# Seven-product units for the first two input blocks of the up projections, with turned blocks gated by wider operations

## The chip, the cores and the metric

The kernel runs on one core of one Trainium2 chip. The metric is the device time of one execution in microseconds, the median over runs. Alongside it there is one profiled execution, from which the profile's page and trace come. The engines are named as the profile names them: PE (TensorE, matrix products), PEld (its weight loads), DVE (VectorE), ACT (ScalarE), POOL (GpSimd) and SP (SyncE, which here only issues DMAs).

## The reference

Two decoder layers over 256 tokens of width 2048, in float32. Each layer has a mixer and then a gated feed-forward part; the change touches only the feed-forward part, which runs once in each layer:

```python
D_MODEL = 2048; SEQ = 256; DEPTH = 2
FFN_HIDDEN = 5632                       # 44 blocks of 128; w_up has 2 * 5632 columns

def conv_ffn(h, w_up, conv_w, conv_b, w_down):
    seq = h.shape[1]
    z = h @ w_up
    zp = jnp.pad(z, ((0, 0), (CONV_WIDTH - 1, 0), (0, 0)))
    z = sum(conv_w[j] * zp[:, j:j + seq] for j in range(CONV_WIDTH)) + conv_b
    a, b = jnp.split(z, 2, axis=-1)
    return (jax.nn.silu(a) * b) @ w_down

    # in each layer: x = x + mixer(...);  h = rms_norm(x, ffn_norm[l]);  x = x + conv_ffn(h, ...)
```

So there are 2048 x 11264 weights up and 5632 x 2048 weights down in each layer, a causal convolution of width 3 along the tokens in between (three taps and a bias for each of the 11264 columns), and the product of the silu of one half with the other half.

## The kernel before, in words

**Products.** Every large product is done with operands split in two: a weight tile `w` of 128 x 1024 values arrives by DMA (SP issues it), ACT writes its rounded part `wh` (line 186), and DVE writes the rest, `wl = w - wh` (line 187). Activations are kept split the same way. One product is then three matmuls: high by high, high by low, low by high (lines 380, 382, 383). A weight tile covers four blocks of 128 output columns and two input blocks of 128 rows; below it is called a piece. For a piece PE runs 12 matmuls of 512 columns: two halves of the tokens, two input blocks, three matmuls each. `project_four` runs through the pieces of one group of four output blocks: 8 pieces for an up projection (16 input blocks), 6 for a full step of the down projection (12 input blocks), into two banks of PSUM.

**Seven-product units.** The generator `seven` (lines 410 to 475) treats two groups of output blocks together, for the first two input blocks: a product of 2 x 2 blocks by 2 x 2 blocks made with 7 products instead of 8. With three matmuls a product, a unit has 21 matmuls where the two pieces it replaces have 24. It pays for that elsewhere. DVE makes sums and differences of the weights (lines 448 to 451, into the tiles `near` and `far`, named `sums` in the trace). Three and a half tiles are split into `wh` and `wl` instead of two. ACT copies one partial result from bank to bank (line 457) and one to the spare tile `p5` (line 462, `p` in the trace). DVE twice adds this spare to a bank (lines 465 and 470). Sums of the activations, made once for two input blocks by `combos` (lines 391 to 407, tile `comb`), must be ready. The second weight tile, `near` and `far` lie where the residual `x` was; `x` is sent to HBM from POOL's queue by the first `combine` of a layer, and fetched back behind the last unit (`x_back`). The generator is advanced one stage at a time between pieces of another projection: `project_four` takes it as `inset`, with the index of the first piece that a stage stands before. Before the change only the down projections use units: two for each of the three full steps, 6 in a layer.

**The feed-forward part.** `ffn` runs 11 up pairs (`up`): four blocks of the first half of the columns (`za`), then the matching four blocks of the second half (`zb`), each by `four`. `STEPS` says after how many up pairs a down step follows: 4 pairs, down over 12 hidden blocks, 3 pairs, down, 4 pairs, down, and a last down over the remaining 8 blocks. A down step has four groups of output blocks (`q` 0 to 3).

**After an up projection** the result has tokens in rows and must be turned. ACT evacuates the two banks into two `z` tiles (line 1422, with the norm's scale), DVE transposes 32 x 32 blocks within them into `tmp` (line 483), 16 DMAs, alternating between SP's and POOL's queues, carry the pieces to `zt` (line 492), and then `conv` works on each of the four turned blocks. ACT computes tap 2 and the bias (line 1436), DVE adds tap 1 and tap 0 (lines 1437 and 1438). For the `a` half ACT applies silu (line 98, tile `conv`); for the `b` half DVE multiplies by it (line 1460), ACT writes the rounded part of the hidden block (line 500) and DVE the rest (line 502).

**What sets the order.** These followers are generators. `tick()` advances all those in flight by one stage, once for each piece (and twice in a unit), so their instructions are sown between the pieces; the generator of a turned group waits 8 ticks (`LATE`) between the transposes' DMAs and `conv`. `held` keeps an instruction from being placed ahead of the latest `wh` or `wl`. A scheduler then fixes the order on each engine, and each engine works strictly in that order. ACT and DVE run ahead of PE as far as the buffers allow: `w` has 5 buffers and `wh` and `wl` have 3 each, with two more of each in a second pool that some pieces use.

## Time and profile before

| | |
|---|---|
| three runs | 2163.55, 2165.5, 2167.18 us; median 2165.5 |
| profiled execution | 2161.98 us, its span 2160.2 us, granted clock 1.000 |
| PE busy | 2152.4 us, 100%; 10700 matmuls recorded |
| PEld busy | 1887.7 us, 87% |
| DVE busy | 1683.7 us, 78%; 2451 instructions |
| ACT busy | 1338.6 us, 62%; 1942 instructions |
| DMA | 491.99 MB, mean 228 GB/s |

A row of the grouped view gives line, engine, operation, the tiles written and read, their shape, the count, then busy time and mean duration of one, then the idle time just before them on their engine and what ended it. The durations of neighbouring instructions overlap a little on DVE and ACT, and by almost half on PE: a matmul is shown with 379 ns, but the next starts after 216 ns. What a matmul costs is therefore read from the distance of starts.

### The profile page before, as it was taken

The numbers are of one execution on the slowest core, as the hardware profiler recorded it, in microseconds if no ns is written. First come the engines' busy times: TensorE is split into PE (matmuls) and PEld (weight loads), VectorE is DVE, ScalarE is ACT, GpSimd is POOL, SyncE is SP. The second block draws the span as 40 slices with busy tenths as digits, with TensorE's granted clock in tenths as the row PEclk, the third lists the DMA queues.
The fourth block names the chain that finished last, engine by engine and source line by source line (L and its number), as shares of the span: only waits on it lengthen the run. The fifth ranks groups of instructions, "written<-read, shape, count | busy, mean of one in ns | idle before, by whom it ended". The sixth has DMA issues, their size and how long they took to land.

```text
span 2160.2 us, 32319 instructions
## 1 busy us (share of the span) xinstructions
PE 2152.4 (100%) x10700; PEld 1887.7 (87%) x10700; DVE 1683.7 (78%) x2451; ACT 1338.6 (62%) x1942; POOL 476.6 (22%) x873
## 2 busy tenths in 40 slices
PE   9999999999999999999999999999999999999999
PEld 8888888888888888888888888888888888888888
DVE  7887768878677867787987787877878578858786
ACT  6677766666656645664565556766666566556652
POOL 0352231212012002111233443212211011011203
PEclk9999999999999999999999999999999999999999
DMA  8755778877777767777777766788786777677786
GB/s 302 224 169 174 224 223 266 250 228 221 231 225 226 216 217 209 249 218 239 243 236 228 241 207 209 224 255 252 235 247 203 229 224 228 217 214 216 223 281 186
DMA packets 494344, 491.99 MB, mean 228 GB/s; under 512 B 115584, under 2 KB 460304, under 8 KB 494048
## 3 DMA queue, kind: packets, MB, share of 16 engines
q1 hardware_dynamic: 466752, 457.60, 67.4%
q0 software_dynamic: 25984, 30.18, 5.8%
q10 hardware_dynamic: 1440, 2.15, 0.4%
q8 instruction: 84, 1.38, 0.3%
q14 instruction: 84, 0.69, 0.1%
HBM read 439.44 MB, written 6.31 MB: 206 GB/s over the span
## 4 chain that ended last, share of the span: by engine, by line
PE 94%; DVE 2%; DMA 1%; SPq 1%; ACT 1%; issue 1%; DVEq 0%; ACTq 0%
PE pm L382 15%; PE pm L380 15%; PE pm L383 15%; PE px L380 10%; PE px L382 10%; PE px L383 10%; PE pm L351 5%; PE pm L352 4%; PE pm L353 4%; PE pm L237 1%; PE pm L316 1%; SPq L492 1%; DVE wl L187 1%; PE pm L319 1%; PE pm L326 0%
## 5 line engine op out<-in xcount | busy, mean ns | idle before, releaser
L187 DVE TENSOR_TENSOR wl<-w,wh 128x1024 fp32r<-128x1024 f32 (+1 forms) x808 | 974.9, 1216 | 354.5 <-ACT wh L186 345.5
L186 ACT ACTIVATE wh<-w 128x1024 fp32r<-128x1024 f32 (+1 forms) x808 | 842.1, 1049 | 515.3 <-PE pm L383 206.2
L492 POOL DMA_DIRECT2D zt<-tmp x413 | 223.5, 549 | 1112.9 <-DVE tmp L483 908.6
L382 PE MATMUL pm<-wl,a 128*128 128x512 f32 x1024 | 388.4, 379 | 0.6 <-DVE wl L187 0.6
L380 PE MATMUL pm<-wh,a 128*128 128x512 f32 x1024 | 388.9, 380 | 0.0
L383 PE MATMUL pm<-wh,a 128*128 128x512 f32 x1024 | 388.1, 379 | 0.0
L380 PE MATMUL px<-wh,a 128*128 128x512 f32 x704 | 266.8, 379 | 0.0
L382 PE MATMUL px<-wl,a 128*128 128x512 f32 x704 | 266.8, 379 | 0.0
L383 PE MATMUL px<-wh,a 128*128 128x512 f32 x704 | 266.8, 379 | 0.0
L382 PEld LDWEIGHTS pm<-wl,a 128*128 128x128 f32 x1024 | 193.5, 189 | 28.6 <-DVE wl L187 1.5
L380 PEld LDWEIGHTS pm<-wh,a 128*128 128x128 f32 x1024 | 193.6, 189 | 27.5
L383 PEld LDWEIGHTS pm<-wh,a 128*128 128x128 f32 x1024 | 193.5, 189 | 27.4
L351 PE MATMUL pm<-wh,a 128*128 128x512 f32 x416 | 158.5, 381 | 0.0
L352 PE MATMUL pm<-wl,a 128*128 128x512 f32 x416 | 157.7, 379 | 0.0
L353 PE MATMUL pm<-wh,a 128*128 128x512 f32 x416 | 157.7, 379 | 0.0
L383 PEld LDWEIGHTS px<-wh,a 128*128 128x128 f32 x704 | 133.1, 189 | 18.9
L380 PEld LDWEIGHTS px<-wh,a 128*128 128x128 f32 x704 | 133.1, 189 | 18.9
L382 PEld LDWEIGHTS px<-wl,a 128*128 128x128 f32 x704 | 133.1, 189 | 18.9
L1436 ACT ACTIVATE conv<-zt,pp 128x256 f32<-128x256 f32 x176 | 100.1, 589 | 71.8 <-DMA zt<-tmp 54.9
L492 POOL DMA_DIRECT2D turn<-tmp x159 | 86.4, 551 | 189.5 <-DVE tmp L483 169.0
L1437 DVE SCALAR_TENSOR_TENSOR conv<-zt,pp,conv 128x255 f32<-128x255 f32 x176 | 83.1, 479 | 53.2 <-ACT conv L1436 44.8
L382 PE MATMUL px<-wl,hid 128*128 128x512 f32 x304 | 115.3, 379 | 0.2 <-DVE wl L187 0.2
(320 smaller groups left out, 3504.8 us busy)
## 6 DMA issues: line engine op xcount, KB each, us to landing
w<-in_w_up SPq DMA_DIRECT2D x352, 512.0 KB, 5.3
w<-in_w_dn SPq DMA_DIRECT2D x164, 512.0 KB, 5.2
w<-in_w_cqkv SPq DMA_DIRECT2D x96, 512.0 KB, 5.0
w<-in_w_abo SPq DMA_DIRECT2D x32, 512.0 KB, 4.8
w<-in_w_cg SPq DMA_DIRECT2D x32, 512.0 KB, 5.0
w<-in_w_co SPq DMA_DIRECT2D x32, 512.0 KB, 4.8
zt<-tmp SPq DMA_DIRECT2D x416, 32.0 KB, 2.3
zt<-tmp POOLq DMA_DIRECT2D x413, 32.0 KB, 2.3
```

What stands on the lines that cost most here:

```text
L186: r = deep["wh"] = SC.activation(wh, w, AF.Copy)
L187: deep["wl"] = V.tensor_tensor(wl, w, wh.bitcast(F32), ALU.subtract)
L237: deep["last"] = PE.matmul(to_two(ps[g][T]), a[:, o + T * P:o + (T + 1) * P], by_two(t, i), start=k + i + j == 0, stop=k + i == KT - 1 and ...
L351: PE.matmul(to_two(ps[T]), ah, h, start=k + i == 0, stop=False)
L352: PE.matmul(to_two(ps[T]), ah, l, start=False, stop=False)
L353: deep["last"] = PE.matmul(to_two(ps[T]), al, h, start=False, stop=k + i == KT - 1)
L380: PE.matmul(to_rows(ps[T]), ah, h, start=not begun and k + i == ks[0], stop=False, skip_group_check=loose)
L382: PE.matmul(to_rows(ps[T]), ah, l, start=False, stop=False, skip_group_check=loose)
L383: deep["mm"] = deep["last"] = PE.matmul(to_rows(ps[T]), al, h, start=False, stop=not more and k + i == ks[-1] + 1, skip_group_check=loose)
L492: queues[(a + b) % len(queues)].dma_start(dst[BLK * b:BLK * (b + 1), :, a * n:(a + 1) * n], tmp[BLK * a:BLK * (a + 1), b * 4 * n:(b + 1) * ...
L1436: held(SC.activation(c, z, AF.Identity, bias=pp[:, cb:cb + 1], scale=w(2)))
L1437: V.scalar_tensor_tensor(c[:, 1:], z[:, :S - 1], w(1), c[:, 1:], ALU.mult, ALU.add)
```

## The change

Two things are changed, both in `ffn`.

First, the up pairs use units too. From the third pair on, the first two input blocks of `za` and `zb` of a pair are computed together by one `seven` unit (`begin_up`), whose stages are inset into the `zb` projection of the pair before it, or into the last group of the down step before it. `four` then starts at the third input block, into the banks that the unit has begun. That is pairs 2 to 10, so 9 units a layer, 18 in the program. Since the tile `comb` has one buffer, the activation sums are made anew whenever the use goes from hidden blocks to the normed input or back: `combine(None)` is for the input, `combine(k)` for hidden blocks. That makes 6 a layer, where there were 3. The first `combine(None)` of a layer, which sends `x` away, now runs as soon as the norm's scale is known and no longer waits for hidden blocks. The units that start a down step stay as they were.

Second, what follows the turning is regrouped. ACT computes tap 0 of each block into `tmp` (new line 1437), which is free by then; DVE adds tap 1 for each block as before (now line 1438), and tap 0 for all four blocks by one addition of 4 x 254 columns (line 1440). Silu, the product with the other half (line 1462), the rounded part (line 1466) and the rest (line 1468) are each one operation on 4 x 256 columns. The `conv` tiles are now two of 1024 columns (before: six of 256), the hidden tiles five of four blocks (before: twenty of one).

```diff
-        def four(j0, inset=None):
-            ps = project_four(w_up[l, j0:j0 + 4], A, KT, inset=inset)
+        def four(j0, inset=None, ps=None):
+            ps = project_four(w_up[l, j0:j0 + 4], A, KT, ks=range(2 if ps else 0, KT, 2), ps=ps, inset=inset)
...
-        def conv(z, j, half):
...
-            c = hp.tile([P, S], F32, tag="conv", name=nm("conv"), bufs=6)
-            held(SC.activation(c, z, AF.Identity, bias=pp[:, cb:cb + 1], scale=w(2)))
-            V.scalar_tensor_tensor(c[:, 1:], z[:, :S - 1], w(1), c[:, 1:], ALU.mult, ALU.add)
-            V.scalar_tensor_tensor(c[:, 2:], z[:, :S - 2], w(0), c[:, 2:], ALU.mult, ALU.add)
+        def conv(z4, tmp, j):
+            c = hp.tile([P, 4, S], F32, tag="conv", name=nm("conv"), bufs=2)
+            far = tmp.rearrange("p (m t) -> p m t", m=4)
+            for i in range(4):
...
+                held(SC.activation(ci, z, AF.Identity, bias=pp[:, cb:cb + 1], scale=w[2]))
+                SC.activation(far[:, i], z, AF.Copy, scale=w[0])
+                V.scalar_tensor_tensor(ci[:, 1:], z[:, :S - 1], w[1], ci[:, 1:], ALU.mult, ALU.add)
+                yield
+            held(V.tensor_tensor(c[:, :, 2:], c[:, :, 2:], far[:, :, :S - 2], ALU.add), "wl")
             return c
...
-                for i in range(4):
-                    a = conv(za[:, i], j0 + i, 0)
-                    act(a, a, AF.Silu)
-                    ca.append(a)
-                    yield
+                a = yield from conv(za, ta, j0)
+                yield
+                held(act(a, a, AF.Silu))
+                ca.append(a)
...
-                for i in range(4):
-                    b = conv(zb[:, i], HT + j0 + i, 1)
-                    V.tensor_tensor(b, b, ca[i], ALU.mult)
-                    t = hp.tile([P, 512], F32R, tag="hid", name=nm("hid"), bufs=20)
-                    split(t, b, turn=True)
-                    hid.append(t)
-                    yield
+                b = yield from conv(zb, tb, HT + j0)
+                yield
+                held(V.tensor_tensor(b, b, ca[0], ALU.mult), "wl")
+                t = hp.tile([P, 4, 512], F32R, tag="hid", name=nm("hid"), bufs=5)
...
+                SC.activation(h, src, AF.Copy)
+                yield
+                held(V.tensor_tensor(lo, src, h.bitcast(F32), ALU.subtract), "wl")
+                hid.extend(t[:, i] for i in range(4))
...
-            yield from combos(t, hid[k:k + 2], hp.tile([P, 1024], F32, tag="tmp", name=nm("tmp"), bufs=2), None)
+            yield from combos(t, A[0:2] if k is None else hid[k:k + 2],
+                              hp.tile([P, 1024], F32, tag="tmp", name=nm("tmp"), bufs=2), None)
...
+        def begin_up(j):
+            return begin([w_up[l, o:o + 4] for o in (4 * j, HT + 4 * j)], None, lambda: A[0:2])
...
+                    elif q == 3 and after:
+                        coming, gen = begin_up(j0)
                         inset = (gen, 0, True)
...
-                    if after:
+                    if after:
+                        queue.append(combine(None))
+                    else:
                         x_back()
-                    else:
-                        queue.append(combine(k0 + n))
...
+            until = sum(n for n, _ in STEPS[:g + 1]) + ahead
+            while j0 < until:
+                now_begun, begun, inset = begun, (), None
+                if j0 + 1 == until:
+                    queue.append(combine(k0))
+                    begun, gen = begin_down(0, k0)
                     inset = (gen, 2, True)
-                up(4 * j0, inset)
+                elif j0:
+                    begun, gen = begin_up(j0 + 1)
+                    inset = (gen, 2, True)
+                up(4 * j0, inset, now_begun)
                 j0 += 1
```

The prediction speaks of three places in the order of instructions; they stand here before and after.

On PE, at the first two input blocks of an up group (`a_3572` and `a_3595`; `pm` and `px` are the PSUM banks): before, the third pair's `za` begins with a plain piece.

```order
L380 MATMUL pm_4777<-wh_4785,a_3572 128x512
L382 MATMUL pm_4777<-wl_4786,a_3572 128x512
L383 MATMUL pm_4777<-wh_4785,a_3572 128x512
L380 MATMUL pm_4777<-wh_4785,a_3595 128x512
L382 MATMUL pm_4777<-wl_4786,a_3595 128x512
L383 MATMUL pm_4777<-wh_4785,a_3595 128x512
L380 MATMUL pm_4778<-wh_4785,a_3572 128x512
L382 MATMUL pm_4778<-wl_4786,a_3572 128x512
L383 MATMUL pm_4778<-wh_4785,a_3572 128x512
L380 MATMUL pm_4778<-wh_4785,a_3595 128x512
L382 MATMUL pm_4778<-wl_4786,a_3595 128x512
L383 MATMUL pm_4778<-wh_4785,a_3595 128x512
```

Now that pair's first two blocks come from a unit between the pieces of the pair before. This is its longest stage, three products; the first has the activation sums (`comb`), the second the first weight tile again, and the third adds to the bank that the unit's first stage began.

```order
L435 MATMUL px_4667<-wh_4695,comb_4251 128x512
L436 MATMUL px_4667<-wl_4696,comb_4251 128x512
L437 MATMUL px_4667<-wh_4695,comb_4251 128x512
L435 MATMUL pm_4664<-wh_4668,a_3595 128x512
L436 MATMUL pm_4664<-wl_4669,a_3595 128x512
L437 MATMUL pm_4664<-wh_4668,a_3595 128x512
L435 MATMUL pm_4665<-wh_4695,comb_4251 128x512
L436 MATMUL pm_4665<-wl_4696,comb_4251 128x512
L437 MATMUL pm_4665<-wh_4695,comb_4251 128x512
```

Two pieces like the first, 24 matmuls, became seven products like these, 21 matmuls, in stages of 1, 3, 1 and 2 products with a piece ahead of each later stage.

On DVE, from the piece ahead of a unit's weight sums (`sums`) to the piece behind them. Before, in the fourth pair, whose unit begins the down step:

```order
L187 TENSOR_TENSOR wl_5430<-w_5428,wh_5429 128x1024
L502 TENSOR_TENSOR hid_5396<-conv_5391,hid_5396 128x256
L1460 TENSOR_TENSOR conv_5420<-conv_5420,conv_5218 128x256
L448 TENSOR_TENSOR sums_4594<-sums_4593,w_5417 128x4x128
L449 TENSOR_TENSOR sums_4595<-sums_4593 128x4x128
L502 TENSOR_TENSOR hid_5425<-conv_5420,hid_5425 128x256
L450 TENSOR_TENSOR sums_4594<-sums_4595,w_5417 128x4x128
L483 STREAM_TRANSPOSE tmp_5339<-z_5341 128x512
L451 TENSOR_TENSOR sums_4595<-w_5417,sums_4594 128x4x128
L483 STREAM_TRANSPOSE tmp_5339<-z_5342 128x512
L187 TENSOR_TENSOR wl_5452<-w_5450,wh_5451 128x1024
```

Now, in the same pair (`w_5411` is the unit's first weight tile, `tmp_5344` the turned group that has just been evacuated, `tmp_5175` holds tap 0 of the group before it):

```order
L187 TENSOR_TENSOR wl_5419<-w_5417,wh_5418 128x1024
L483 STREAM_TRANSPOSE tmp_5344<-z_5346 128x512
L1438 SCALAR_TENSOR_TENSOR conv_5368<-zt_5176,pp,conv_5368 128x255
L448 TENSOR_TENSOR sums_4249<-sums_4248,w_5411 128x4x128
L483 STREAM_TRANSPOSE tmp_5344<-z_5347 128x512
L449 TENSOR_TENSOR sums_4250<-sums_4248 128x4x128
L1440 TENSOR_TENSOR conv_5368<-conv_5368,tmp_5175 128x4x254
L450 TENSOR_TENSOR sums_4249<-sums_4250,w_5411 128x4x128
L451 TENSOR_TENSOR sums_4250<-w_5411,sums_4249 128x4x128
L187 TENSOR_TENSOR wl_5445<-w_5443,wh_5444 128x1024
L187 TENSOR_TENSOR wl_5466<-w_5411,wh_5465 128x1024
L1462 TENSOR_TENSOR conv_5368<-conv_5368,conv_5132 128x1024
```

Single blocks' operations gave way to the long ones of lines 1440 and 1462, of which one stands among the sums and one behind the unit's first split; lines 448 to 451 and 483 stand as before.

On ACT, from the split of a unit's third tile (`far`, read as `sums`) past the two bank copies, again in the fourth pair. Before:

```order
L186 ACTIVATE wh_5536<-sums_4595 128x1024
L457 ACTIVATE pm_5468<-pm_5469 128x512
L98 ACTIVATE conv_5531<-conv_5531 128x256
L1436 ACTIVATE conv_5544<-zt_5340,pp 128x256
L98 ACTIVATE conv_5544<-conv_5544 128x256
L462 ACTIVATE p_889_5169<-px_5471 128x512
L186 ACTIVATE wh_5550<-w_5549 128x1024
```

Now:

```order
L186 ACTIVATE wh_5532<-sums_4250 128x1024
L457 ACTIVATE pm_5461<-pm_5462 128x512
L1436 ACTIVATE conv_5528<-zt_5345,pp 128x256
L1437 ACTIVATE tmp_5344<-zt_5345,pp 128x256 x3
L462 ACTIVATE p_889_5199<-px_5464 128x512
L186 ACTIVATE wh_5544<-w_5543 128x1024
L186 ACTIVATE wh_5561<-sums_4248 128x4x128
```

Between the copies of lines 457 and 462 two silu operations have gone, which wait for DVE, and three taps have come; the split of the next piece still follows line 462.

More of the change, by code (lines that the diff above doesn't have):

```diff
@@ L1507, in finish_x @@
                 nxt.feed(m)
-        comb, right = [None, None], [None]
+        comb, right = [-1, None], []
         away = [(t, c0, dp.tile([P, 4, S], F32, tag=f"xs{c0}", name=nm("xs"))) for t, c0, n in xload]
         def combine(k):
-            while len(hid) < k + 2:
-                yield
-            if k == 0:
-                while not (norm.Rt is not None):
+            if k is not None:
+                while len(hid) < k + 2:
+                    yield
+            elif not right:
+                while norm.Rt is None:
                     yield
@@ L1531, in x_back, with begin @@
                     part[c0 + i] = (t, i, c0 + 3)
-        def begin(q, k0):
+        def begin(w4s, k, acts):
             got = []
@@ L1540, in sums @@
             def sums():
-                while comb[0] != k0:
+                while comb[0] != k:
                     tick()
@@ L1545, in begin, with begin_down @@
             spare = hp.tile([P, 512], F32, tag="z", name=nm("p5"), bufs=2)
-            return got, seven([w_dn[l, 4 * (q + i):4 * (q + i) + 4] for i in range(2)], lambda: hid[k0:k0 + 2],
-                              lambda: comb[1], k0 * P, banks4, sums, spare)
+            return got, seven(w4s, acts, lambda: comb[1], (k or 0) * P, banks4, sums, spare)
+        def begin_down(q, k):
+            return begin([w_dn[l, 4 * (q + i):4 * (q + i) + 4] for i in range(2)], k, lambda: hid[k:k + 2])
+        def begin_up(j):
+            return begin([w_up[l, o:o + 4] for o in (4 * j, HT + 4 * j)], None, lambda: A[0:2])
         def down(k0, n, first, final, begun, after):
-            acts = hid[k0:k0 + n]
+            acts, coming = hid[k0:k0 + n], ()
             if final and last:
@@ L1568, in down @@
                     if q == 0:
-                        later, gen = begin(2, k0)
+                        later, gen = begin_down(2, k0)
                         inset = (gen, 2, False)
                     elif q == 1:
+                        inset = (gen, 0, True)
+                    elif q == 3 and after:
+                        coming, gen = begin_up(j0)
                         inset = (gen, 0, True)
@@ L1587, in down @@
                     add_y(q, True)
+            return coming
         j0, k0, hid = 0, 0, []
-        queue.append(combine(0))
-        begun = None
+        queue.append(combine(None))
+        begun = ()
         for g, (now, ahead) in enumerate(STEPS):
-            while 4 * j0 < k0 + 4 * (now + ahead):
-                inset = None
-                if 4 * (j0 + 1) >= k0 + 4 * (now + ahead):
-                    begun, gen = begin(0, k0)
+            until = sum(n for n, _ in STEPS[:g + 1]) + ahead
[4 more added lines that the diff above has]
+                    begun, gen = begin_down(0, k0)
                     inset = (gen, 2, True)
-                up(4 * j0, inset)
+                elif j0:
+                    begun, gen = begin_up(j0 + 1)
+                    inset = (gen, 2, True)
+                up(4 * j0, inset, now_begun)
                 j0 += 1
@@ L1602, in ffn @@
                 tick()
-            down(k0, n, g == 0, final, begun, g == len(STEPS) - 2)
+            begun = down(k0, n, g == 0, final, begun, j0 < HT // 4)
             k0 += n
```

20 lines of the change are left out of this document (11 added, 9 removed).

## The prediction

> **What bounds the kernel now.** I read the page first, then PE's waits, then PE's instructions in order of time around one of today's units, and then busy time by stretches.
>
> ```profile
> PE 2152.4 (100%) x10700; PEld 1887.7 (87%) x10700; DVE 1683.7 (78%) x2451; ACT 1338.6 (62%) x1942; POOL 476.6 (22%) x873
> PE 94%; DVE 2%; DMA 1%; SPq 1%; ACT 1%; issue 1%; DVEq 0%; ACTq 0%
> ```
>
> PE is busy for all but 8 us of a span of 2160.2, and 94% of the chain of waits is PE. The next question is what PE waits for, in the view of waits of PE alone:
>
> ```profile
> PE px L435 <- DVE pm L465: 1.0, 1, 1.0
> PE pm L382 <- DVE wl L187: 1.0, 3, 0.4
> PE px L382 <- DVE wl L187: 0.2, 1, 0.2
> ```
>
> Columns: total, times, longest. Twelve units and over 800 splits cost PE 2.2 us. So this kernel is as long as its matmuls, and time goes down with their number as long as DVE and ACT keep their lead. What a matmul costs is the distance between starts, here through a unit of the fourth pair of layer 0 (lines of the timeline of PE; start, duration):
>
> ```profile
> 512.43 0.38 PE L380 MATMUL pm<-wh,a 128*128 128x512 f32 x1
> ...
> 518.69 0.38 PE L437 MATMUL pm<-wh,comb 128*128 128x512 f32 x1
> ...
> 521.49 0.38 PE L435 MATMUL pm<-wh,comb 128*128 128x512 f32 x1
> ...
> 522.36 0.38 PE L382 MATMUL pm<-wl,a 128*128 128x512 f32 x1
> ...
> 524.51 0.38 PE L383 MATMUL pm<-wh,a 128*128 128x512 f32 x1
> ```
>
> There are 57 matmuls from the first to the last of these lines: 12.08 us for 56 steps, 0.2157 us each, with no gap.
>
> **The matmuls removed.** A new unit has 21 matmuls for 24; 18 units take away 54. 54 x 0.2157 = 11.65 us. This is the whole gain, for the bytes loaded stay the same (the unit reads the same two weight tiles).
>
> One rule of the Trainium skill reads PE otherwise. Perfetto Trace Analysis, Identifying the Most-Contended Engine, says that matmul busy time misleads and that weight-load busy time is one of the good measures. By the page's row that is 87%, so 54 matmuls would be worth 0.87 x 11.65 = 10.2 us, and the result 1.5 us later. The trace does not show the spare 13%: starts stand evenly 0.2157 us apart.
>
> **What DVE gains and loses.** Groups of the whole run (count | busy us, mean ns | idle before):
>
> ```profile
> L187 DVE TENSOR_TENSOR wl<-w,wh 128x1024 fp32r<-128x1024 f32 (+1 forms) x808 | 974.9, 1216 | 354.5 <-ACT wh L186 345.5 <-DMA zt<-tmp 5.4
> L1438 DVE SCALAR_TENSOR_TENSOR conv<-zt,pp,conv 128x254 f32<-128x254 f32 x176 | 82.2, 478 | 2.2
> L502 DVE TENSOR_TENSOR hid<-conv,hid 128x256 fp32r<-128x256 f32 x88 | 41.5, 482 | 3.3 <-ACT hid L500 3.3
> L187 DVE TENSOR_TENSOR wl<-sums,wh 128x1024 fp32r<-128x1024 f32 (+1 forms) x36 | 37.6, 1045 | 5.1 <-ACT wh L186 4.9
> L1460 DVE TENSOR_TENSOR conv<-conv,conv 128x256 f32<-128x256 f32 x88 | 35.7, 417 | 0.0
> L448 DVE TENSOR_TENSOR sums<-sums,w 128x512 f32<-128x512 f32 x12 | 8.0, 669 | 0.0
> L395 DVE TENSOR_TENSOR tmp<-hid 128x256 f32<-128x256 f32 x12 | 4.4, 403 | 0.0
> L465 DVE TENSOR_TENSOR pm<-px,p 128x512 f32<-128x512 f32 x6 | 4.2, 695 | 2.8 <-PE px L437 1.8 <-ACT p L462 1.0
> L407 DVE TENSOR_TENSOR comb<-tmp,comb 128x512 fp32r<-128x512 f32 x6 | 4.1, 679 | 0.0
> ```
>
> - Gone: lines 1438 (tap 0), 502 and 1460, 82.2 + 41.5 + 35.7 = 159.4 us.
> - In their place 88 operations of 1024 columns (44 additions of tap 0, 22 products, 22 rests). The trace has none of these forms; the nearest is the split, 974.9 / 808 = 1.21 us: 106 us.
> - Each unit: four sums at 0.67, two additions to a bank at 0.695, and splits of three sums tiles (37.6 / 12 = 3.13) and one whole tile in place of two: 2.67 + 1.39 + 1.93 = 6.0 us, 18 times: 108 us.
> - Six more sets of activation sums, two at 0.403, four smaller and one at 0.679, at most 3.1 us each: 19 us.
>
> Together +73 us: 1757 us, 82% of the new span. On average there is cover.
>
> **ACT**, from the same view:
>
> ```profile
> L186 ACT ACTIVATE wh<-w 128x1024 fp32r<-128x1024 f32 (+1 forms) x808 | 842.1, 1049 | 515.3 <-PE pm L383 206.2 <-PE px L383 148.8 <-PE pm L353 69.0
> L1436 ACT ACTIVATE conv<-zt,pp 128x256 f32<-128x256 f32 x176 | 100.1, 589 | 71.8 <-DMA zt<-tmp 54.9 <-DMA w<-in_w_up 15.5 <-issue 1.2
> L500 ACT ACTIVATE hid<-conv 128x256 fp32r<-128x256 f32 x88 | 46.6, 535 | 40.7 <-DVE conv L1460 40.5
> L98 ACT ACTIVATE conv<-conv 128x256 f32<-128x256 f32 x88 | 35.7, 411 | 21.2 <-DVE conv L1438 20.7
> L186 ACT ACTIVATE wh<-sums 128x1024 fp32r<-128x1024 f32 (+1 forms) x36 | 32.7, 908 | 24.4 <-PE pm L383 10.7 <-PE px L383 7.8 <-DVE wl L187 3.1
> L510 ACT ACTIVATE a<-x,pp 128x256 fp32r<-128x256 f32 x32 | 15.0, 497 | 8.5 <-DVE x L1483 7.7 <-DMA x<-in_x 0.8
> L462 ACT ACTIVATE p<-px 128x512 f32<-128x512 f32 x6 | 3.5, 588 | 0.1
> ```
>
> The tap on ACT isn't in the trace. It lies between line 98 (no column of scales, 0.411) and line 1436 (scale and bias, 0.589); I take line 510, a scale from `pp` alone, 0.497: 176 x 0.497 = 87 us (72 to 104). Gone are lines 500 and 98, 82 us; in their place 44 operations of 1024 columns at 842.1 / 808 = 1.04, 46 us. Units: 32.7 / 12 + 1.04 - 2.08 of splits and two bank copies at 0.59, 2.9 us, 18 times 52. Activation sums, 6 x 0.6 = 4. Together +107: 1446 us, 67%. ACT's largest idle time is behind PE (206 + 149 + 69 of 515 us): it had filled all buffers and waited. That is the cover.
>
> **One pair closely.** Busy time by stretches, for the third pair (no unit inset) and the fourth (with one) of layer 0:
>
> ```profile
> core 0: us, PE busy (x) PEld busy (x) DVE busy (x) ACT busy (x) POOL busy (x), PEclk, DMA share, GB/s
> 441.40:482.90 41.50, 41.50 (x194) 36.33 (x193) 32.36 (x47) 26.90 (x39) 8.65 (x16) 1.00 0.78 238
> 482.90:528.80 45.90, 45.90 (x214) 40.21 (x213) 38.46 (x54) 29.90 (x43) 8.66 (x16) 1.00 0.76 231
> ```
>
> A pair of the new kind loses 8 x 0.467 + 4 x 0.472 + 4 x 0.406 = 7.3 us of DVE, gains 4 x 1.21 = 4.8, and its unit adds 6.0: 32.4 + 3.5 = 35.9 us within 41.5 - 0.65 = 40.8 us of PE, 88%. Today's pair with a unit has 84% and goes without a gap in PE; it leaves 7.4 us unused, the new one 4.9. What was an exception becomes the rule, for 18 pairs.
>
> **The tight place** is line 465: DVE must stop there until PE has ended the unit's third product, and the split of the next piece stands behind it (timeline of DVE, idle time in brackets):
>
> ```profile
> 519.17 0.70 DVE L465 TENSOR_TENSOR px<-pm,p 128x512 f32<-128x512 f32 x1 [1.19 <-PE pm L437]
> 519.95 1.23 DVE L187 TENSOR_TENSOR wl<-w,wh 128x1024 fp32r<-128x1024 f32 x1
> ```
>
> This split ends at 521.18; PE wants it at 522.36 (above). Whatever the lead was, it is 1.2 us here, and PE needs the addition itself at 521.49, 1.6 us after its end. Once, in the third step's unit, that was not enough (DVE, ACT and PE):
>
> ```profile
> 932.66 1.22 DVE L187 TENSOR_TENSOR wl<-w,wh 128x1024 fp32r<-128x1024 f32 x1 [1.49 <-ACT wh L186]
> 933.81 0.69 DVE L465 TENSOR_TENSOR pm<-px,p 128x512 f32<-128x512 f32 x1
> 931.27 0.42 ACT L98 ACTIVATE conv<-conv 128x256 f32<-128x256 f32 x1 [1.13 <-DVE conv L1438]
> 934.55 0.48 PE L435 MATMUL px<-wh,comb 128*128 128x512 f32 x1 [1.03 <-DVE pm L465]
> ```
>
> There the split stood ahead of line 465, and its `wh` was held up by silu operations. In the new order such silus no longer stand between ACT's two copies: three taps (1.5 us) do, which wait for nothing more than the tap before them. That is near the old 0.4 + 0.6 + 0.4 with its wait of 1.13, so I do not make the new units worse than the old ones, nor better. What the unit adds behind line 465 is as before, one split. For the price of the 18 new ones I take the old rate, 2.2 us in 12 units at most: 0.18 each, 3.3 us. The bounds are 0 and the one bad case every time, 18 x 1.03 = 18.5 us.
>
> The other wait that stays is ACT's for the turned block:
>
> ```profile
> 443.00 1.24 ACT L1422 ACTIVATE z<-pm,Rt 128x512 f32<-128x512 f32 x2
> 455.40 1.09 ACT L1436 ACTIVATE conv<-zt,pp 128x256 f32<-128x256 f32 x2 [5.17 <-DMA zt<-tmp]
> ```
>
> 12.4 us from evacuation to `conv`. It eats lead that ACT has to spare, as it did here without a gap in PE. The taps stand behind it and add 2 us a group to ACT; queued behind them are splits. The store of `x` merely moves ahead within the layer, while no unit runs. I cost both at nothing; were the lead gone, they would show in the rate per unit above.
>
> **The sum.** Profiled span 2160.2 - 11.65 + 3.3 = 2151.9; the execution around it is 1.8 longer (2161.98), 2153.6; the median of the runs stands 3.5 above that execution: **2157 us**, 8.4 below 2165.5.
>
> **The rivals.**
> - *Most of the gain goes into gaps at the units.* The steady 88% leaves DVE less time to catch up between one unit and the next, so line 465 is reached late. Against it: in the unit above DVE came 1.19 us early. At half a microsecond for each new unit, 9 us: 2163, no change that can be told. Chance 0.17.
> - *Long operations in the way.* A block of 1.21 us where 0.47 stood makes whatever comes next on DVE up to 0.74 us late; if every unit lost that, 13 us: 2167, no change. Against it: in the order no long operation stands between line 465 and the split behind it, and DVE waits ahead of line 465. Beside it stands the Trainium skill: Perfetto Trace Analysis, Optimizing Scalar/DVE Operations, advises breaking instructions up where these engines aren't saturated but leave gaps on others; no run here shows it yet. Chance 0.06.
> - *DVE becomes the bound, slower.* In the pair with a unit DVE is idle for 45.9 - 38.46 = 7.4 us. If that is all real waiting (on ACT, DMA and line 465), a new pair needs 35.9 + 7.4 = 43.3 us against 40.8: 2.5 us, 18 times 45 us, 2199. It decides from 4.9 us of true waiting in a pair; at 5.9 it is 18 us lost, 2172. For it: no row shows how much of the idle time is slack. Against it: PE had no gap in that very pair. Chance 0.11.
>
> **How the numbers follow.** The forecast, with 0 to 6 us of gaps, has 0.66. A measurement of this kernel can tell about 0.2%, 4.3 us, from no change: faster is below 2161.2, slower above 2169.8. Faster: 0.66 and a part of the first rival, 0.71. Slower: the third rival and a little of the second, 0.12. The rest, 0.17, is no change. The lower end is no new gap and the old 2.2 us gone as well: 2165.5 - 11.65 - 2.2 = 2152. The upper end takes in the first rival and half of the second, 2166; outside are the third rival and small remainders.
>
> **What would show it.** PE starts 0.216 us apart and 54 fewer of them; PE's waits at lines 435 and 382 together 4 to 7 us; DVE near 1757 and ACT near 1446 us busy. I am wrong if PE's waits exceed 8 us, or if its starts spread over whole pairs; a PE gap at splits and not at line 465 would speak for the third rival.

## The result: 1.3% slower

The changed kernel takes 2193.0 us, the median of four runs (2186.8 to 2198.4), against 2166.3 for the kernel before on the same chip. That is 27 us slower by the medians; the ratio is 1.0129 (28 us), with a 95% interval of 1.0117 to 1.0141. The forecast was 2157, 8 us faster. The profiled execution took 2194.9 us, its span 2193.1.

From the page of the changed kernel, the engines and the chain of waits:

```profile
PE 2158.5 (98%) x10646; PEld 1879.4 (86%) x10646; DVE 1750.2 (80%) x2373; ACT 1428.8 (65%) x2064; POOL 480.6 (22%) x873
PE 72%; DVE 10%; DMA 9%; SPq 4%; issue 3%; ACT 2%; DVEq 0%; POOL 0%; ACTq 0%; POOLq 0%
```

The 54 matmuls are gone (10700 before), but PE is busy for 6 us more, and its part in the chain of waits has fallen from 94% to 72%. DVE, DMA and SP's queue now have 23%. The waits of PE in the changed kernel come first; under them stand the waits of ACT for transfers, in the changed kernel and then in the kernel before (total us, times, longest; smaller ones left out):

```profile
PE pm L382 <- DVE wl L187: 8.7, 11, 2.3
PE px L435 <- ACT px L457: 8.5, 2, 4.7
PE px L382 <- DVE wl L187: 6.3, 8, 1.6
PE pm L435 <- ACT pm L457: 3.6, 3, 2.6
PE pm L435 <- DVE px L465: 0.7, 2, 0.4
```

```profile
ACT wh L186 <- DMA w<-in_w_up: 55.4, 32, 4.5
ACT conv L1436 <- DMA zt<-tmp: 38.4, 21, 5.7
ACT wh L186 <- DMA w<-in_w_dn: 34.1, 30, 3.4
```

```profile
ACT conv L1436 <- DMA zt<-tmp: 54.9, 23, 5.4
ACT wh L186 <- DMA w<-in_w_dn: 13.2, 16, 2.8
ACT wh L186 <- DMA w<-in_w_up: 9.9, 8, 1.9
```

PE now waits 27 us at splits and at ACT's copy of line 457; at line 465, the place that the prediction watched, it waits 1 us. In its splits (line 186) ACT waits four times as long for weight tiles as before, 90 us for 23.

A ledger of start distances closes the sum. Every distance between two matmuls above the usual 0.216 us counts as lost: 7.3 us in the kernel before, 51.1 in the changed one. Of these, 18.7 us lie behind splits, 12.9 behind line 457, 7.5 in stretches of half clock, and 9.1 in 94 small delays. 51.1 - 7.3 - 11.65 = 32 us, close to the difference of the two profiled executions (2194.9 - 2162.0 = 33).

**One gap, followed back.** It lies at the unit that is inset in the second pair behind the first down step of layer 0, an up unit that was not there before. Rows of SP's queue, ACT, DVE and PE (start, duration, idle time and what ended it in brackets):

```profile
628.98 7.67 SPq L199 DMA_DIRECT2D w<-in_w_up  x2
643.18 6.00 SPq L492 DMA_DIRECT2D zt<-tmp  x8
649.28 1.08 SPq L199 DMA_DIRECT2D w<-in_w_up  x2
650.41 0.51 SPq L445 DMA_DIRECT2D w<-in_w_up  x1
650.96 0.51 SPq L445 DMA_DIRECT2D sums<-in_w_up  x1
651.56 11.18 SPq L199 DMA_DIRECT2D w<-in_w_up  x4
660.02 1.06 ACT L186 ACTIVATE wh<-w 128x1024 fp32r<-128x1024 f32 x1 [2.58 <-DMA w<-in_w_up]
661.12 1.23 DVE L187 TENSOR_TENSOR wl<-w,wh 128x1024 fp32r<-128x1024 f32 x1 [2.91 <-ACT wh L186]
662.26 1.56 DVE L483 STREAM_TRANSPOSE tmp<-z 128x512 f32<-128x512 f32 x2
...
667.09 0.69 DVE L451 TENSOR_TENSOR sums<-w,sums 128x512 f32<-128x512 f32 x1
667.70 2.35 DVE L187 TENSOR_TENSOR wl<-w,wh 128x1024 fp32r<-128x1024 f32 x2
668.98 0.48 PE L382 MATMUL pm<-wl,a 128*128 128x512 f32 x1 [1.42 <-DVE wl L187]
```

SP issues nothing from 636.65 to 643.18, and then the transfers of a turned block for 6.0 us; two plain loads, the unit's two tiles and the next plain load stand behind them. That load is issued at 651.56 and used at 660.02, 8.5 us later. ACT has been idle for 2.6 us by then, DVE for 2.9. Then comes DVE's densest stretch: two transposes, a tap, the four sums and the addition of line 1440, 5.4 us from 662.26 to 667.70 without a split. PE, whose lead was spent on the wait, stops at the split behind it. DVE's idle time and its work fall one after the other instead of side by side; a busy share of 80% says nothing of that.

The kernel before had the same order of issues at its units, and its load behind the unit's tiles, issued at 492.53 and used at 500.01, took 7.5 us. But ACT came to it with all buffers full, held only by PE, and 1.7 us did no harm:

```profile
490.61 1.06 ACT L186 ACTIVATE wh<-w 128x1024 fp32r<-128x1024 f32 x1 [1.53 <-PE px L383]
...
500.01 1.06 ACT L186 ACTIVATE wh<-w 128x1024 fp32r<-128x1024 f32 x1 [1.67 <-DMA w<-in_w_up]
```

**The gaps at line 457** come from late transfers too, those of turned blocks. At the first new unit of layer 0 the transposes are done at 425.9, SP sends its eight transfers from 425.98, and POOL its last two only at 431.67 [2.16 <-issue], among five loads of 512 KB that SP issues from 431.21:

```profile
425.98 5.12 SPq L492 DMA_DIRECT2D zt<-tmp  x8
431.21 3.59 SPq L199 DMA_DIRECT2D w<-in_w_up  x5
431.67 1.10 POOL L492 DMA_DIRECT2D zt<-tmp  x2 [2.16 <-issue]
437.44 0.60 ACT L1436 ACTIVATE conv<-zt,pp 128x256 f32<-128x256 f32 x1 [5.67 <-DMA zt<-tmp]
439.69 0.57 ACT L457 ACTIVATE pm<-pm 128x512 f32<-128x512 f32 x1
440.32 0.48 PE L435 MATMUL pm<-wh,a 128*128 128x512 f32 x1 [2.61 <-ACT pm L457]
```

ACT stands 5.7 us at line 1436, two taps and a split follow, and the copy that PE wants comes behind them. The two longer gaps at line 457, which end at 867.5 and 1577.9, look the same: ACT stands 5.3 and 6.9 us at line 1436, until the last of POOL's transfers, issued among SP's loads, has landed. The three make up 11.6 of the 12.9 us.

### The profile page after: what moved, and what is told of

Same layout as the page of the kernel before. It is cut to its first block, busy times and chain, and to the rows that moved or that the text cites. A ratio compares the mean times of both kernels' runs of the same rounds, so it can differ in the third digit from the quotient of the medians.

```text
span 2193.1 us, 32450 instructions
## 1 busy us (share of the span) xinstructions
PE 2158.5 (98%) x10646; PEld 1879.4 (86%) x10646; DVE 1750.2 (80%) x2373; ACT 1428.8 (65%) x2064; POOL 480.6 (22%) x873
## 3 DMA queue, kind: packets, MB, share of 16 engines
q10 hardware_dynamic: 1440, 2.15, 0.3%
## 4 chain that ended last, share of the span: by engine, by line
PE 72%; DVE 10%; DMA 9%; SPq 4%; issue 3%; ACT 2%; DVEq 0%; POOL 0%; ACTq 0%; POOLq 0%
PE pm L382 11%; PE pm L380 11%; PE pm L383 11%; DMA w<-in_w_up 6%; PE px L382 5%; PE px L383 5%; PE px L380 5%; DVE wl L187 5%; PE pm L351 4%; PE pm L353 4%; PE pm L352 4%; SPq L492 3%; DMA w<-in_w_dn 2%; DVE tmp L483 1%; PE pm L237 1%
## 5 line engine op out<-in xcount | busy, mean ns | idle before, releaser
L187 DVE TENSOR_TENSOR wl<-w,wh 128x1024 fp32r<-128x1024 f32 (+1 forms) x790 | 950.4, 1217 | 319.1 <-ACT wh L186 317.4
L186 ACT ACTIVATE wh<-w 128x1024 fp32r<-128x1024 f32 (+1 forms) x790 | 818.2, 1049 | 466.8 <-PE pm L383 132.5
L382 PE MATMUL pm<-wl,a 128*128 128x512 f32 x952 | 364.2, 383 | 8.2 <-DVE wl L187 8.2
L380 PE MATMUL pm<-wh,a 128*128 128x512 f32 x952 | 363.1, 381 | 0.1
L383 PE MATMUL pm<-wh,a 128*128 128x512 f32 x952 | 361.9, 380 | 0.0
L382 PE MATMUL px<-wl,a 128*128 128x512 f32 x632 | 241.5, 382 | 5.6 <-DVE wl L187 5.5
L380 PE MATMUL px<-wh,a 128*128 128x512 f32 x632 | 240.3, 380 | 0.0
L383 PE MATMUL px<-wh,a 128*128 128x512 f32 x632 | 240.0, 380 | 0.0
L380 PEld LDWEIGHTS pm<-wh,a 128*128 128x128 f32 x952 | 180.5, 190 | 26.3 <-ACT wh L186 0.5
L383 PEld LDWEIGHTS pm<-wh,a 128*128 128x128 f32 x952 | 180.8, 190 | 25.4
L351 PE MATMUL pm<-wh,a 128*128 128x512 f32 x416 | 158.5, 381 | 0.0
L352 PE MATMUL pm<-wl,a 128*128 128x512 f32 x416 | 157.7, 379 | 0.0
L353 PE MATMUL pm<-wh,a 128*128 128x512 f32 x416 | 157.7, 379 | 0.0
L382 PEld LDWEIGHTS px<-wl,a 128*128 128x128 f32 x632 | 119.9, 190 | 27.5 <-DVE wl L187 10.7
L380 PEld LDWEIGHTS px<-wh,a 128*128 128x128 f32 x632 | 120.0, 190 | 17.2
L383 PEld LDWEIGHTS px<-wh,a 128*128 128x128 f32 x632 | 119.7, 189 | 16.8
L187 DVE TENSOR_TENSOR wl<-sums,wh 128x1024 fp32r<-128x1024 f32 (+1 forms) x90 | 94.2, 1046 | 26.8 <-ACT wh L186 26.8
```

The source lines that it names most:

```text
L186: r = deep["wh"] = SC.activation(wh, w, AF.Copy)
L187: deep["wl"] = V.tensor_tensor(wl, w, wh.bitcast(F32), ALU.subtract)
L351: PE.matmul(to_two(ps[T]), ah, h, start=k + i == 0, stop=False)
L352: PE.matmul(to_two(ps[T]), ah, l, start=False, stop=False)
L353: deep["last"] = PE.matmul(to_two(ps[T]), al, h, start=False, stop=k + i == KT - 1)
L380: PE.matmul(to_rows(ps[T]), ah, h, start=not begun and k + i == ks[0], stop=False, skip_group_check=loose)
```

## Experiments

Each was timed beside the kernel before; "against before" is the difference of the medians on one chip. By this measure the change itself is at +26.7.

| run | us | against before | ratio, 95% interval |
|---|---|---|---|
| regroup_only | 2167.2 | +2.8 | 1.0013 (1.0004 to 1.0023) |
| units_only | 2187.7 | +23.2 | 1.0110 (1.0094 to 1.0127) |
| no_sums | 2177.1 | +12.7 | 1.0062 (1.0047 to 1.0077) |
| unit_loads_pool | 2176.4 | +11.9 | 1.0062 (1.0047 to 1.0077) |
| pool_no_sums | 2175.4 | +11.4 | 1.0049 (1.0032 to 1.0066) |
| pool_late12 | 2173.0 | +8.9 | 1.0040 (1.0025 to 1.0055) |
| pool_spread | 2182.9 | +18.8 | 1.0085 (1.0068 to 1.0101) |
| zt_on_gpsimd | 2223.5 | +59.5 | 1.0279 (1.0263 to 1.0294) |
| pool_units_only | 2194.3 | +29.6 | 1.0135 (1.0120 to 1.0150) |
| pool_alt | 2167.7 | +3.1 | 1.0019 (1.0009 to 1.0028) |
| pool_copy_vector | 2178.6 | +13.9 | 1.0061 (1.0046 to 1.0076) |
| sums_on_gpsimd | 2208.9 | +44.2 | 1.0203 (1.0188 to 1.0218) |
| pool_no_copy | 2171.4 | +7.8 | 1.0036 (1.0025 to 1.0048) |
| alt_sync | 2176.6 | +12.9 | 1.0059 (1.0044 to 1.0074) |
| pool_alt_late12 | 2171.0 | +7.3 | 1.0033 (1.0023 to 1.0042) |
| before_pool | 2161.8 | -1.9 | 0.9990 (0.9980 to 0.9999) |
| pool_first_old | 2168.7 | +4.8 | 1.0022 (1.0013 to 1.0031) |
| pool_first | 2164.8 | +0.9 | 1.0009 (1.0000 to 1.0018) |

The theories at the start: A, weight loads come late at the units; B, DVE comes late behind a unit's sums; C, the long operations and ACT's taps stand in the way.

**Which half of the change.** One run keeps the regrouped followers and drops the units, the other the reverse.

```diff
-        def up(j0, inset=None, begun=()):          # regroup_only, in the loops of before
-            pa, pb = begun or (None, None)
+        def up(j0, inset=None):
+            pa = pb = None
```

> The kernel before with the regrouped followers alone (tap 0 on ScalarE, operations of 1024 columns), and no unit in the up pairs. Theory A (late weight loads at the units): the regrouping costs nothing by itself, 2164 to 2168 us, PE's waits stay near 2 us. Theory B (vector engine late behind a unit's sums): the same. Theory C (long operations and taps in the way, whatever the units do): 2172 us or more, with waits of PE at splits all over the up pairs.

> The change with its units in the up pairs, but the followers as before (three taps as before, operations on 256 columns). Theory C: without the long operations the loss is gone, 2160 us or less. Theories A and B: the units are the cause, so the loss stays; the vector engine has some 53 us more to do than in the change, so 2195 to 2205 us.

Regrouping alone costs 2.8 us (0.9 to 5.0 by the interval), and units alone 23 of the 27. C falls as the main cause: the loss comes with the units. But units_only lies between its two expectations: DVE is busy there for 36 us more than in the change (1786 for 1750), and the kernel is 5 us faster, so the sum of DVE's work alone does not set the time.

**The sums, and the queue of the loads.**

```diff
-        then(V.tensor_tensor(block(near, 0), block(b2, 0), block(b1, 0), ALU.subtract))   # and the other three
+        if not lo: near = far = b2                                                         # no_sums
-            in_order("w", nc.sync.dma_start(w.rearrange("p (m c) -> p m c", m=4), src))
+            nc.gpsimd.dma_start(w.rearrange("p (m c) -> p m c", m=4), src)                 # unit_loads_pool
```

> The change, but in the up pairs' units the four weight sums on VectorE are left out (the second weight tile is split in their place), so the output is not the reference's; loads, splits and matmuls stay. Theory B: the waits of PE at the split behind the sums (15 us) go, and with them most of the half-clock stretches: 2170 us or less. Theory A: the loads are as late as they were, so at most 5 us are gained: 2187 us or more.

(The edit acts on all units whose first input block is block 0: 18 up and four down, 88 operations.)

> The change, but the two weight tiles of every unit are fetched through GpSimd's queue and not through SyncE's, so that they neither wait behind the turning DMAs there nor hold up the next plain weight tiles. Theory A (by queue order): ScalarE's waits for weight tiles fall from 90 us to under 40 and the time to 2175 us or less. Theory A (by the memory's rate or the buffer that a unit's tile holds) and theory B: no change within 5 us, 2188 to 2198.

Each takes away 14 to 15 of the 27 us, so A and B both have a part, and neither the whole. (In unit_loads_pool the unit's loads also lose their fixed place in the order of the plain loads, which `in_order` gave them; the two effects are not told apart.) PE's waits with the loads moved, and then without the sums:

```profile
PE pm L435 <- ACT pm L457: 5.7, 4, 3.8
PE px L382 <- DVE wl L187: 4.8, 4, 2.8
PE px L435 <- ACT px L457: 4.2, 7, 1.5
PE pm L382 <- DVE wl L187: 1.9, 3, 0.9
```

```profile
PE pm L435 <- ACT pm L460: 5.7, 3, 5.0
PE px L435 <- ACT px L460: 5.4, 1, 5.4
PE pm L382 <- DVE wl L187: 2.1, 3, 0.9
PE px L382 <- DVE wl L187: 0.3, 1, 0.3
```

The waits at splits fall from 15.0 to 6.7 and 2.4 us. Those at the copy of line 457 (460 in the second kernel) stay, 12.1 before the edits and 9.9 and 11.1 after. ACT's wait for weight tiles fell to 46 us with the loads moved, not below the 40 that A had asked for.

**Both at once, and the rest.**

> The change with both edits tried so far: the two tiles of each unit fetched through GpSimd's queue, and the four weight sums left out (in the 18 up units and in the four first down units, 88 operations; the products take a fetched tile in their place, so the output is not the reference's). Each edit alone brought the time from 2193 to 2176-2177. If late loads (A) and the sums (B) are two separate causes that add up, 2193 - 17 - 16 = 2160, between 2156 and 2164. If they are one and the same slack, so that either edit takes away what the other would, 2173 to 2178. If a third cause D (ScalarE's copy of line 457 held behind a gate or fill step that waits for its transposed tile zt) makes up the rest, the waits of TensorE for line 457, 11 to 12 us in both runs before, stay at 8 us or more and the time stays above 2164.

The two don't add up: 2175.4 (2167.7 to 2179.4), at the level of either alone. (Its profiled execution is the fastest of its five, 2167.7; there PE lost 23.1 us by the ledger, 8.6 of them at the copy.) So either edit takes away much of what the other would. That left D, the copy behind ACT's wait for zt. Three runs went for it, all with the loads on GpSimd's queue:

```diff
-LATE = 8
+LATE = 12                                                                        # pool_late12
-        SC.activation(x1, x0, AF.Copy)
+        V.tensor_copy(x1, x0)                                                     # pool_copy_vector
+        if lo: SC.activation(x1, x0, AF.Copy)                                     # pool_no_copy
```

> The change with the units' tiles fetched through GpSimd's queue, and the wait between a transposition and its convolution longer by four steps (LATE 12 for 8). D (ScalarE held by zt at lines 1436 and 1437): ScalarE's wait for zt falls from about 60 us to under 25, TensorE's waits for line 457 from 11.6 us to under 4, the stretches of halved clock behind them go too, and the time falls from 2176 to 2160-2167. If D does not count, 2173 to 2180. Since hid comes later by four steps, a wait of the down part for it could cost some: above 2180.

> The change with the units' tiles fetched through GpSimd's queue, and the copy x1 <- x0 of line 457 made by VectorE instead of ScalarE, in all 30 units. D (ScalarE held by zt ahead of this copy): TensorE's waits for line 457, 9.9 us before, fall under 3 us and the time from 2176 to 2163-2169. If the copy is late on either engine, because both stand behind the same late work, 2173 to 2182.

> The change with the units' tiles fetched through GpSimd's queue, and the copy of line 457 left out in the 22 units whose first input block is block 0 (the second sum then starts from nothing: a part of the product is left out, and the output is not the reference's). This measures the wait for the copy by itself. If it is a cost of its own: TensorE's waits there (9.9 us, with halved clock behind some of them) go, and the time falls from 2176 to 2162-2167. If it is only the first place where a lateness shows, the unit's next waits (lines 462 and 465) take it over: 2172 to 2180.

None reached the time that D forecast. With LATE 12 the copy still costs 8.7 us (5.2 and 3.5 in the view of waits) and the time falls by 3. But this run did not take D away. ACT's largest wait for zt, with the loads moved and then with LATE 12 as well:

```profile
ACT conv L1436 <- DMA zt<-tmp: 55.9, 29, 4.6
ACT tmp L1437 <- DMA zt<-tmp: 74.4, 32, 5.3
```

Line 1437, the tap that `held` does not bind, now stands first in all 44 groups (in 2 of them without LATE 12), and in the median it starts 10.0 us after the evacuation, where the first operation started after 10.2. So on ACT the convolution did not come later, and ACT's wait for zt grew. On DVE the copy is late as well:

```profile
PE pm L435 <- DVE pm L457: 8.0, 7, 2.4
PE px L435 <- DVE px L457: 6.2, 6, 1.8
```

Left out in 22 units, the copy saves 4 to 5 us of the 12 that remained: 2171.4, just under the upper of the two expectations. The eight copies that stay in down units still cost 4.4 us, line 465 costs 2.2 (1.1 before), and splits 7.6 (6.7 before). So the copy seems to be partly a cost of its own and partly the first place where lateness shows.

**Where the sums stand, and who makes them.**

```diff
+        if not lo: yield; tick()                    # pool_spread: between the second and the third sum
-                    inset = (gen, 2, True)
+                    inset = (gen, 1, True)          # and the unit begins one step earlier
+        e, put = (V, then) if lo else (nc.gpsimd, lambda r: r)    # sums_on_gpsimd, loads as in the change
```

> The change with the units' tiles fetched through GpSimd's queue, the unit begun one step earlier, and its four weight sums in two pairs with a step between them, so that no 5.4 us of sums stand in one piece ahead of a split. B as a matter of where the sums stand: TensorE's waits for splits fall from 7.9 us to under 4 and the time to 2164-2171. B as a matter of VectorE's total work: no change, 2173 to 2180. A and D alone: no change.

> The change with the four weight sums of the 22 units whose first input block is block 0 (18 up, 4 down) made by GpSimd instead of VectorE, all that is computed kept, the loads in SyncE's queue as in the change. B as VectorE's time: as with the sums left out, 2172 to 2182, and less if GpSimd is quick enough. If GpSimd's sums (1.59 us for 128x256 at line 705, so perhaps 3 us for one of 512 columns and 12 us for four) come late for the products or hold back the transfers of zt that GpSimd issues, 2187 to 2215.

Spread out they do more harm, 7 us over unit_loads_pool, with 18 us of waits at splits; whether by the place of the sums or by the earlier start, this run does not tell. On GpSimd they are worse still. PE's longest waits are there at the copy (line 458 in that kernel), 26.8 us, and not at splits, 7.7; the sums stand in GpSimd's queue ahead of its transfers of zt and wait for the unit's tiles, which may be why, but no run separates it. And DVE gets little back: its busy time falls from 1750 to 1734 us, though 88 sums of 0.68 us, 60 us, have left it. One reason stands in the rows (POOL and DVE at the same time):

```profile
418.90 1.27 POOL L450 TENSOR_TENSOR sums<-sums 128x512 f32<-128x512 f32 x1
420.25 2.31 POOL L451 TENSOR_TENSOR sums<-sums,w 128x512 f32<-128x512 f32 x1
421.34 2.30 DVE L1441 TENSOR_TENSOR conv<-conv,tmp 128x1016 f32<-128x1016 f32 x1
```

The addition on DVE takes 2.30 us beside a sum on GpSimd (1.20 in the changed kernel), and the sum 2.31 beside DVE's work for 1.27 alone. The 62 splits on DVE that overlap such a sum take 1.62 us in the mean, the other 780 of 1024 columns take 1.22. With line 1439 (12 taps of 1.05 us for 0.48) and line 1441 (four additions) that accounts for some 37 of the 44 us by which DVE's busy time did not fall. The Trainium skill, Perfetto Trace Analysis, Optimizing Scalar/DVE Operations, says that the two engines share an SBUF read port, so that moving work between them might not help; this trace agrees.

**SyncE held by the turned blocks.**

```diff
-                transposed(lambda T: z[T], tmp, zt)
+                transposed(lambda T: z[T], tmp, zt, (nc.gpsimd,))       # zt_on_gpsimd
```

> The change with all 16 transfers of a transposed up tile issued by GpSimd, none by SyncE; the units' own loads stay in SyncE's queue. If A works through SyncE being held by the transfers of zt (which wait for VectorE's transposes) so that the loads behind them are issued late: as with the units' loads moved, 2172 to 2180, ScalarE's waits for w under 50 us (90 in the change). If A works by the two tiles more that stand ahead of the next plain load in one queue: 2187 to 2197. A side effect either way: zt lands later by the longer chain of GpSimd's issues, and the waits for zt grow (D).

2223: neither. With sixteen issues in a row on one queue zt comes later (from the evacuation to the first operation on the turned block ACT takes 17.7 us in the median, 9.9 in the change), and weight loads are no earlier for it, since ACT's wait for tiles of `w_up` rises from 55 to 76 us. So this run does not tell which of the two ways makes SP's order cost time.

**The loads moved, but the old followers.**

> The 7-product units of the up projections with the old followers (no grouped 1024-column operations, no tap on ScalarE), and the units' tiles fetched through GpSimd's queue. In the run with units alone TensorE lost nothing at line 457 (no tap on ScalarE ahead of the copy) but 9 us at line 465 and 19 us behind splits. If the late loads and ScalarE's hold at line 457 (D) are what is left to remove, 2158 to 2168. If VectorE's total work (1786 us with the old followers against 1750) sets the gaps, 2172 to 2182, with the waits at line 465 and behind splits staying at 15 us or more.

2194: here the other queue helped nothing (2187.7 through SP). ACT's waits for zt rose from 54.9 to 91.7 us, probably because half of the transfers of zt share GpSimd's queue with the unit's loads. If so, the move of the loads trades one blocked queue for another, and whether that pays depends on what is late.

**How many units.** The next runs leave out three of the nine units of a layer, those right behind another inside a group, with the loads on either queue; one more leaves only the two a layer that begin inside a down step; and one moves the loads in the kernel before.

```diff
-                elif j0:
+                elif j0 % 2:            # pool_alt, alt_sync, pool_alt_late12 (12 units)
+                elif False:             # pool_first, pool_first_old (4 units)
```

> The change with the units' tiles fetched through GpSimd's queue and three of the nine units of a layer left as full products, those that come right behind another unit inside a group (12 units stay, 36 matmuls or 7.8 us fewer than before). If each unit costs the same (about 24 us lost over 18 units, 1.3 us each), 12 x 1.3 - 7.8 = 8 us above before, 2170 to 2175. If units cost more where they follow one another (the sums of the one fall among the followers of the other), 2156 to 2166.

> The change with three of the nine units of a layer left as full products (12 units stay), and the loads in SyncE's queue as in the change. With the loads through GpSimd this was 2168, 8 us under the 18 units. If crowding and SyncE's order are separate costs: 2193 - 8 = 2185, between 2180 and 2189. If the crowding is what makes SyncE's order cost anything (loads catch up where a pair without a unit follows): 2166 to 2174.

> 12 units, their tiles fetched through GpSimd's queue, and the convolution four steps later behind its transposes (LATE 12 for 8). The run with 12 units lost 10.5 us at line 457, most of it where ScalarE's line 1436 waits for zt. If four steps are enough to take that wait away: 2156 to 2162, under the kernel before (2165). If, as with 18 units, the wait only moves (4 us less there): 2163 to 2168.

> The kernel before with the tiles of its 12 down units fetched through GpSimd's queue: how far the change of queue acts without the up units. The kernel before lost only 7 us at all gaps, so it can gain at most that: 2160 to 2167 by every theory; above 2168, GpSimd's queue has a cost of its own that the runs with it also carry.

> The kernel before with the units' tiles fetched through GpSimd's queue (2161.8 by itself, 1.9 us under before) and only those up units that are begun inside a down part, two a layer (4 units, 12 matmuls or 2.6 us fewer), with the old followers. If a unit that stands alone is hidden as the down units are: 2158 to 2160.5, the fastest kernel of all. If every up unit costs its 0.9 us: 2162 to 2164.

> The same four up units with the change's grouped followers. Grouping alone cost 2 to 3 us with the old units. If units that stand alone are hidden: 2159 to 2163. If every up unit costs its 0.9 us: 2163 to 2167.

Loss for each up unit is the time against before plus 0.65 us of matmuls saved for each unit, over the number of units. Through SP's queue it is 2.1 us with 18 units and 1.7 with 12; through GpSimd's 1.3, 0.9 and, with four, 0.9. (Grouping's +2.8 and the queue's -1.9 are still in these; if they add up, four units lose 2.6 us, as much as they save.) So a unit costs more the denser they stand, and not even the sparsest show a gain. pool_alt and alt_sync fell between their two expectations: crowding and SP's order are neither quite separate costs nor one. With the loads on GpSimd's queue the grouped followers help the units (11.9 against 29.6 us with 18 of them, 0.9 against 4.8 with four); through SP's queue they don't (26.7 against 23.2). LATE 12 did no good with 12 units: ACT's wait for zt fell there from 57 to 29 us, and PE's waits at line 457 from 10.4 to 5.5, but its waits at splits rose from 1.8 to 7.0. before_pool, with no up unit, is the fastest kernel, by 0.1%; its interval just excludes no change.

## Why the prediction was wrong

- **Matmuls removed: right.** 10646 for 10700, and starts still 0.216 us apart where PE runs freely; 11.65 us were gained.
- **Work of DVE and ACT: right.** 1750 us for 1757, 1429 for 1446. The tap took 0.501 (0.497 was taken), the long additions 1.20. Two of the long operations were mis-sized, both in the split of the hidden block: line 1468 on DVE, 1.52 for 1.21, 7 us in all, and line 1466 on ACT, 1.53 for 1.04, 11 us.
- **"The tight place": the step that failed.** Line 465 was no dearer than forecast, 1 us. But the price of the 18 new units was taken from the old ones, 0.18 us each (PE's waits at line 465 and at splits), as though the new ones had as much lead to draw on. The loss against before came to 2.1 us for each, and it lies at splits and at line 457. The upper bound of 18.5 us was drawn from line 465 alone; even with it the sum gives 2172, 21 us short of the result. The prediction's own sign of being wrong, waits of PE above 8 us, showed: 27 us.
- **"The bytes loaded stay the same" and "I cost both at nothing": failed.** The bytes are the same, but the order of the queues is not: the next plain load now stands behind the unit's tiles and behind transfers of zt. Moving the loads gave back 15 us. ACT's wait for zt had lead to eat before; now PE waits 12 us for the copy of line 457, almost all of it where ACT stood for zt ahead of it.
- **"DVE becomes the bound", the third rival with a chance of 0.11, is nearest.** Its range was 2172 to 2199, and its sign was a gap at splits and not at line 465. Its question was whether the idle time of a pair is slack. About one pair of the changed kernel, by stretches:

```profile
661.00:704.30 43.30, 41.88 (x194) 36.13 (x193) 36.97 (x48) 31.42 (x45) 8.69 (x16) 1.00 0.75 230
```

  It has 36.97 us of DVE. DVE idles for 6.3 us in it, and PE stands for 1.4. That its 43.3 us are the number that this rival had worked out (35.9 + 7.4) is luck. From the first matmul of one unit to that of the next, 16 stretches of the trace have 189 matmuls, 40.8 us without a gap; they take 40.8 to 48.9 us, 42.3 in the mean. The six with over 36 us of DVE take 41.6 to 45.2, and DVE idles for 5 to 7 us in each: not all of it is slack, as the rival feared, but it is less than its 7.4. That PE had no gap in the old pair showed only that the lead built up in pairs without a unit still sufficed. What was not foreseen is that DVE idles there because of ACT, and ACT because of transfers (in the stretch above DVE waits for nothing but ACT's `wh`, and ACT longest for weight tiles, 7.5 us). So the bound looks like the chain of the three and not DVE's work. That the four sums' 2.7 us of DVE time are worth almost as much as the loads, and that the two don't add up, fits such a chain; it does not prove it.
- **The second rival** (long operations) was not the main cause: grouping alone cost 3 us.
- **Half clock** was in no rival: 7.5 us.

What stays open: how the remaining 11 us (both edits made) divide between the copy, splits and zt, since no run took ACT's wait for zt away; which way SP's order costs time; and why four units beside old followers cost 5 us.

## What to carry to other kernels

Idle time of a helper engine inside a stage is slack only if the view of waits shows it waiting for the bound engine; where it waits for transfers, work added to it can add to the stage. A price measured on rare units, with easy stretches between them to catch up, must not be multiplied for dense ones: look at what each unit puts ahead of others in every queue, SP's and POOL's too. Where either of two edits helps and both together help no more, the two causes are likely to share one chain. And whether an edit delays what it is meant to delay is read from its own trace, as LATE 12 shows: the wait came back at another line.

## What the runs showed of the hardware

**The clock falls to half behind a short gap.** By stretches, around another gap that ends at 523.0 (PE busy, PEld, DVE, ACT, POOL, then granted clock):

```profile
516.00:520.40 4.40, 4.40 (x22) 3.78 (x20) 4.40 (x7) 3.61 (x5) 1.26 (x3) 1.00 0.49 150
520.40:523.20 2.80, 0.50 (x3) 0.19 (x2) 2.77 (x5) 1.99 (x2) 2.80 (x6) 1.00 0.53 110
523.20:527.20 4.00, 4.00 (x12) 3.20 (x12) 4.00 (x4) 1.89 (x4) 0.28 (x1) 0.57 0.63 150
527.20:530.00 2.80, 2.80 (x15) 2.45 (x14) 2.80 (x4) 2.73 (x6) 0.00 (x0) 1.00 1.05 363
```

Matmuls then start 0.427 us apart for 3.4 us, or 6.8 behind some longer gaps (others of 4 to 5 us were followed by 3.4), so the gap shown costs some 1.7 us more. Over all traces of this study (beyond their first 50 us), with a gap read as the distance of starts beyond 0.216 us, none of 41 gaps from 1.4 to 2.0 us brought this about by itself, and 39 of 43 gaps of 2.1 us or more did. The Trainium skill, TensorE: Matmul & The Clock Gate, Part 1, gives a window of 3.4 us that runs freely and warns of idle gaps above that length; the length of the half-clock stretches agrees, but 22 gaps between 2.1 and 3.3 us were enough here.

**DVE and GpSimd slow each other** when both work on two operands in SBUF (above): 1.62 us for 1.22 in DVE's splits, up to 2.3 for 1.27 in most of GpSimd's sums. DVE's transposes, which read one operand, are not slowed: the 30 that overlap a sum take 0.86 us, the others 0.85.
